# Issuing an output projection in four quarter-width pieces between attention steps instead of two halves at one place

## The chip, the cores and the metric

The kernel runs on one core of one Trainium2 chip. The metric is the device time of one execution in microseconds (us), the median of several runs. The engines are TensorE (PE in the rows: matmuls, with PEld its weight loads), VectorE (DVE), ScalarE (ACT), GpSimd (POOL) and SyncE (SP), which here issues transfers. Each engine executes its own list of instructions in order, and the five lists meet only at semaphores.

## The reference

Two decoder layers on 512 tokens of width 1024, in fp32. Layer 0 mixes tokens by gated linear attention, layer 1 by native sparse attention (16 heads in 4 groups, head width 64). After either mixer comes a mixture of 16 experts. The part at issue is the end of layer 1's mixer and its way into the experts' router:

```python
def nsa_mixer(x, w_in, ..., w_out):
    ...
    o = gb[..., 0:1] * o_cmp + gb[..., 1:2] * o_slc + gb[..., 2:3] * o_win
    ...                                  # o: (B, S, 1024), three branches of attention
    return o @ w_out

for i in range(DEPTH):
    h = gla_mixer(x, ...) if i % 2 == 0 else nsa_mixer(x, ...)
    x = layer_norm(DN_ALPHA * x + h, ln_g[i, 0], ln_b[i, 0])
    f = moe_ffn(x, w_router, ...)        # first step: s = sigmoid(x @ w_router)
    x = layer_norm(DN_ALPHA * x + f, ln_g[i, 1], ln_b[i, 1])
```

## The kernel before, in words

**Tiles.** The 512 tokens are four tiles of 128, numbered 0 to 3. fp32 products are emulated: every operand is split into a high and a low fp16 part, and a product is three matmuls (high by high, high by low, low by high).

**Attention steps.** `nsa_attn` walks a list `order` of 32 steps (tile, group, branch). Steps 0 to 7 are token tile 3, 8 to 15 tile 2, 16 to 23 tile 1, 24 to 31 tile 0. At step i the loop issues `begin(i + 2)`, the scores of the step after next (L1459, L1460: one PSUM bank for each block of keys; when a new tile starts also `cmp_scores`, L1439 to L1446), then for every second step `cmp_pv` (L1494 to L1497, the compressed branch), then `pv` (L1480 to L1485, probabilities by values). `combine` (L1504 to L1516) scales each result by its gate and sums the branches into the tile's output `o`, on VectorE, with the last addition (L1516) on GpSimd for tiles 1 to 3. The probabilities are exponentials by ScalarE (L1427 to L1463) whose low halves VectorE makes (L1435). The buffer `ott`, through which the second and third branch are added, exists once.

**What is filled in.** When a tile's last step is done, its output projection is put in a list `fill`, with the step at which it falls due; the table `ATTN_FILL` holds these steps, one entry for each tile. Three kinds of function are filled in:
- `tr` transposes `o` (TensorE, then the split into fp16 halves oT by ScalarE, L231, and VectorE, L232).
- `out_proj(t, half)` multiplies oT by the 1024 x 1024 output weight, of which one "unit" is 256 columns: units 0 and 1 are the first half of the result's columns, 2 and 3 the second. A unit is the 24 matmuls of `proj_moving` (L256 to L258). After the second unit of a half VectorE adds the residual from PSUM into `r` (L420) and takes the statistics of that half (L291). After the second half follows the layer norm: L310 to L316 on numbers of one column, L302 on both halves, and L303 on both halves, which writes the tile's new rows.
- `finish(t)` is `turn` (eight transposes of the new rows, L273, and their split into xt, L231 and L232) and `score` (the router's logits, L441 to L443: 24 matmuls with 16 columns).

**Priority.** A scheduler may move an instruction a little within an engine's list; the rows in the section on the change show the lists as they come out.

**After attention.** Tile 1's `finish` and all of tile 0's projection belong to the opening of the expert layer, whose weights are split on ScalarE (L178) and VectorE (L180) from the last attention steps on, as they arrive (transfers issued by SyncE at L166 into the buffers that `pv` has released).

The weights' inner loop of one unit:

```python
for k in range(KT):                      # KT = 8
    s = slice(k * 256, (k + 1) * 256)
    nc.tensor.matmul(out, xt[0][:, k], w[0][:, s], start=(k == 0), stop=False)
    nc.tensor.matmul(out, xt[0][:, k], w[1][:, s], start=False, stop=False)
    nc.tensor.matmul(out, xt[1][:, k], w[0][:, s], start=False, stop=(k == KT - 1))
```

Of the kernel before, what the change touches and what calls it, by code (L numbers as in the profile page):

```python
# [34 lines left out]
OUT_POOL = (0, 1), (1, 1), (2, 1)  # L35
PRELUDE = ("r0 r1 o0 t2 r2 oa s2 ob rt rs c0 t3 s3 r3 c1 xb",
           "r0 r1 xa o0 t2 oa s2 r2 rt ob rs c0 t3 s3 r3 c1 xb")
ATTN_FILL = {3: (9, 11, 11, 14), 2: (17, 18, 19, 23), 1: (25, 28, 33), 0: (32,)}
AHEAD = 2
HOT_BY = "ddp"  # L40
UNIT_BY = "dddppppppp"
# [18 lines left out]
class Trunk:  # L60
# [344 lines left out]
    def out_proj(self, t, half, post=True, us=(0, 1)):  # L405
        nc = self.nc
        w, lng, lnb = self.op
        if half == 0:
            self.r = self.xtile(f"r{t}")
            self.bn = self.tmp([P, 2, 6], F32, "bn", 4)  # L410
        r = self.r
        if us[0] == 0:
            self.op_ps = self.bank()
        ps = self.op_ps
        for u in us:
            self.proj_moving(ps[:, u * 256:(u + 1) * 256], w[half * 2 + u], self.oT[t])
        if us[-1] == 0:
            return
        hs = slice(half * 512, half * 512 + 512)
        nc.vector.scalar_tensor_tensor(r[:, hs], ps, IWS / ALPHA, self.x[t][:, hs], op0=OP.mult, op1=OP.add)  # L420
        self.ln_stats(r, half)
        if half == 1:
            self.ln_ins = self.layer_norm(r, lng, lnb)
            self.x[t] = r
            if post:
                self.later(lambda: self.finish(t))
# [989 lines left out]
    def nsa_attn(self, T, pool, early, rest, kcA, kcB, vc, kA, kB, V, VF, qA, qB, gate):  # L1416
# [20 lines left out]
        def cmp_scores(t):  # L1437
            cs = self.bank()
            nc.tensor.matmul(cs.rearrange("p (h q) -> p h q", h=4), self.identb,  # L1439
                             self.cmt[:, t][:, None, :].to_broadcast([P, 4, P]), start=True, stop=False,  # L1440
                             skip_group_check=True)
            for g in range(4):
                gs = slice(g * 32, (g + 1) * 32)
                nc.tensor.matmul(cs[gs], kcA[:, gs], qa(g, t), start=False, stop=False, skip_group_check=True,
                                 tile_position=(0, g * 32))
                nc.tensor.matmul(cs[gs], kcB[:70, gs], qb(g, t), start=False, stop=(g == 3), skip_group_check=True,  # L1446
                                 tile_position=(0, g * 32))
            pc = T([P, S], "pf", F32, 3)
            nc.scalar.activation(pc, cs, AF.Exp)
            pch = T([P, 2, S], "pch", F16, 2)  # L1450
            split(pch[:, 0], pch[:, 1], pc)
            return pch
# [19 lines left out]
        def pv(t, g, b, ph):  # L1472
            ob = self.bank()
            for h in range(4):
                hs = slice(h * P, (h + 1) * P)
                o0 = ob[:, h * 65:(h + 1) * 65]
                exact = t < NT - 1
                if exact:
                    pf = ph[:, t].rearrange("p i q -> p (i q)").bitcast(F32)
                    nc.tensor.matmul(o0, pf[:, hs], VF[b][t][:, g], start=True, stop=(t == 0))  # L1480
                last = t if exact else t + 1
                for j in range(last):
                    nc.tensor.matmul(o0, ph[:, j, 0, hs], V[b][j][:, g, 0:65], start=(j == 0 and not exact), stop=False)
                    nc.tensor.matmul(o0[:, :64], ph[:, j, 0, hs], V[b][j][:, g, 65:129], start=False, stop=False)
                    nc.tensor.matmul(o0, ph[:, j, 1, hs], V[b][j][:, g, 0:65], start=False, stop=(j == last - 1))  # L1485
            return ob

        def cmp_pv(g, pch):
            gs = slice(g * 32, (g + 1) * 32)
            ob = self.bank()  # L1490
            for h in range(4):
                hs = slice(h * P, (h + 1) * P)
                o0 = ob[:, h * 65:(h + 1) * 65]
                nc.tensor.matmul(o0, pch[gs, 0, hs], vc[gs, 0:65], start=True, stop=False, tile_position=(g * 32, 0))  # L1494
                nc.tensor.matmul(o0[:, :64], pch[gs, 0, hs], vc[gs, 65:129], start=False, stop=False,
                                 tile_position=(g * 32, 0))
                nc.tensor.matmul(o0, pch[gs, 1, hs], vc[gs, 0:65], start=False, stop=True, tile_position=(g * 32, 0))  # L1497
            return ob

        def combine(t, g, i, ob, o, first):  # L1500
            cf = T([P, 4], "ocf", F32, 4)
            den = ob[:, 64:260:65]
            if i == 0:
                nc.vector.tensor_scalar(cf, den, 1e-30, None, op0=OP.max)  # L1504
                den = cf
            nc.vector.reciprocal(cf, den)
            nc.vector.tensor_mul(cf, cf, gate[:, t, g * 4:(g + 1) * 4, i])
            og = o[:, g * 256:(g + 1) * 256].rearrange("p (h d) -> p h d", h=4)
            v = ob[:, :260].rearrange("p (h d) -> p h d", h=4)[:, :, 0:64]
            cb = cf[:, :, None].to_broadcast([P, 4, 64])  # L1510
            if first:
                nc.vector.tensor_mul(og, v, cb)
            else:
                tt = T([P, 4, 64], "ott", F32, OTT)
                nc.vector.tensor_mul(tt, v, cb)
                (nc.gpsimd if t else nc.vector).tensor_add(og, og, tt)  # L1516
# [5 lines left out]
        def begin(i):  # L1522
            if i < len(order):
                t, g, b = order[i]
                if g == 0 and b == 0:
                    if t < 3:
                        pch[t] = cmp_scores(t)
                    o[t] = self.row("o")
                ph[i] = scores(t, g, b)

        fill = []
        begin(0)
        begin(1)
        for i, (t, g, b) in enumerate(order):
            begin(i + 2)
            if i in REST_AT:
                for j in range(REST_AT.count(i)):
                    rest[0]()
                    rest = rest[1:]
            if t < 3 and b == 0:  # L1540
                combine(t, g, 0, cmp_pv(g, pch[t]), o[t], True)
            combine(t, g, 1 + b, pv(t, g, b, ph.pop(i)), o[t], t == 3 and b == 0)
            self.pump()
            if i == REST_AT[-1]:
                self.drain()
                ph_, self.ph = self.ph, pool
                early.close()
                self.hl["a"] = self.ctx.enter_context(self.tc.tile_pool(name="wa1", bufs=1, side="right",
                                                                        reuse_waits="tile"))
                self.ph = ph_  # L1550
                self.out_proj_begin([], *self.ln_params(2))
                units = [self.fetch_aside(u) for u in range(3)]
            if i in SPLIT_AT:
                by = SPLIT_BY[SPLIT_AT.index(i)]
                self.op[0].append(self.split(units.pop(0), (), nc.gpsimd if by == "p" else None))
                if i == SPLIT_AT[0]:
                    units.append(self.fetch_aside(3))
            if i == CMP_AT:
                pch[3] = cmp_scores(3)
            if i == 7:  # L1560
                for h in range(4):
                    combine(3, h, 0, cmp_pv(h, pch[3]), o[3], False)
            for f in [f for f in fill if f[0] <= i]:
                fill.remove(f)
                f[1]()
            if i == len(order) - 3:
                self.moe_ahead(1)
            if g == 3 and b == 1:
                def tr(t=t):
                    self.oT[t] = self.transpose_split(o[t], f"oT{t}")  # L1570
                at = ATTN_FILL[t]
                fill.append((at[0], tr))
                if t:
                    fill.append((at[1], lambda t=t: self.out_proj(t, 0)))
                    fill.append((at[2], lambda t=t: self.out_proj(t, 1, False)))
                if t > 1:
                    fill.append((at[3], lambda t=t: self.finish(t)))
        self.table_of(AF.Silu, self.exp_ins)
        for _, f in fill:
            f()  # L1580
# [112 lines left out]
```

## Time and profile before

| | |
|---|---|
| time, median of 3 runs | 957.69 us (957.1 to 959.45) |
| the profiled execution | 958.76 us, span 956.7 us |
| mean granted TensorE clock | 0.965 of full speed |
| busy: TensorE, its weight loads | 92%, 76% |
| busy: VectorE, ScalarE, GpSimd | 78%, 58%, 33% |

The span runs from the first to the last instruction on the chip. Shares are of the span. A busy TensorE means that some matmul is on it. The stretch at issue, from the projection of tile 3 to that of tile 1, lies between 650 and 736 us of the span. Times in the rows are us from the start of the span unless marked ns.

### The profile page before, as it was taken

The numbers are of one execution on the slowest core, as the hardware profiler recorded it, in microseconds if no ns is written. First come the engines' busy times: TensorE is split into PE (matmuls) and PEld (weight loads), VectorE is DVE, ScalarE is ACT, GpSimd is POOL, SyncE is SP. The second block draws the span as 40 slices with busy tenths as digits, with TensorE's granted clock in tenths as the row PEclk, the third lists the DMA queues.
The fourth block names the chain that finished last, engine by engine and source line by source line (L and its number), as shares of the span: only waits on it lengthen the run. The fifth ranks groups of instructions, "written<-read, shape, count | busy, mean of one in ns | idle before, by whom it ended". The sixth has DMA issues, their size and how long they took to land. (4 is left out here: it accounts for less than half of the span.)

```text
span 956.7 us, 26589 instructions
## 1 busy us (share of the span) xinstructions
PE 879.4 (92%) x11218; PEld 722.4 (76%) x11218; DVE 743.5 (78%) x1662; ACT 557.6 (58%) x1178; POOL 313.9 (33%) x353
## 2 busy tenths in 40 slices
PE   6999999996799999879989998999999669999994
PEld 2468888876798889648978886768788568888871
DVE  5972226889899999878678774688777899999967
ACT  4823334424499999713643527775444539999940
POOL 0210021003444331550154524543431258723153
PEclk9999999998899999989999999979999879999997
DMA  8652322072399997951322001120005549999683
GB/s 287 257 210 76 122 89 89 2 307 90 131 367 415 367 377 283 233 178 45 134 89 89 1 3 45 39 97 1 2 2 203 238 176 372 392 382 376 242 155 111
DMA packets 29277, 169.19 MB, mean 177 GB/s; under 512 B 3520, under 2 KB 4160, under 8 KB 12640
## 3 DMA queue, kind: packets, MB, share of 16 engines
q1 hardware_dynamic: 23168, 144.49, 40.1%
q0 software_dynamic: 3072, 12.72, 6.0%
q10 hardware_dynamic: 2912, 10.23, 2.8%
q8 instruction: 90, 1.47, 0.6%
q14 instruction: 35, 0.29, 0.1%
HBM read 153.91 MB, written 13.50 MB: 175 GB/s over the span
## 5 line engine op out<-in xcount | busy, mean ns | idle before, releaser
L851 POOL TENSOR_SCALAR ohe<-icap,rt_px 128x96 f16<-128x96 f32 x112 | 113.1, 1025 | 134.1 <-PE bank L940 125.5
L180 DVE SCALAR_TENSOR_TENSOR whl<-wsu,whl 128x512 f16<-128x512 f32 x192 | 127.0, 711 | 2.9 <-ACT whl L178 2.7
L180 DVE SCALAR_TENSOR_TENSOR whl<-wst,whl 128x512 f16<-128x512 f32 x116 | 75.4, 701 | 68.7 <-ACT whl L178 68.7
L178 ACT ACTIVATE whl<-wsu 128x512 f16<-128x512 f32 x192 | 106.7, 624 | 3.2 <-PE bank L258 3.2
L862 PE MATMUL bank<-ohe,xs 128*128 128x96 f16 x2048 | 99.4, 212 | 6.7 <-DVE ohe L851 5.5
L178 ACT ACTIVATE whl<-wst 128x512 f16<-128x512 f32 x144 | 80.8, 624 | 35.8 <-PE bank L249 9.8
L862 PEld LDWEIGHTS <-xs 128*128 128x128 f16 x2048 | 94.9, 101 | 7.3 <-DVE ohe L851 4.5
L180 DVE SCALAR_TENSOR_TENSOR wha<-wst,wha 128x512 f16<-128x512 f32 x144 | 93.8, 701 | 3.0 <-ACT wha L178 3.0
L256 PE MATMUL bank<-whl,xt 128*128 128x256 f16 x320 | 88.1, 275 | 6.9 <-ACT xt L231 6.9
L257 PE MATMUL bank<-whl,xt 128*128 128x256 f16 x320 | 88.1, 275 | 0.0
L258 PE MATMUL bank<-whl,xt 128*128 128x256 f16 x320 | 87.4, 274 | 0.1
L178 ACT ACTIVATE wha<-wst 128x512 f16<-128x512 f32 x144 | 79.7, 623 | 3.5 <-DMA wst<-moe 3.5
L937 PE MATMUL bank<-xh,whl 128*128 128x96 f16 x576 | 75.2, 206 | 0.0
L935 PE MATMUL bank<-xh,whl 128*128 128x96 f16 x576 | 75.2, 206 | 0.0
L936 PE MATMUL bank<-xh,whl 128*128 128x96 f16 x576 | 75.2, 206 | 0.0
L258 PE MATMUL bank<-whl,oT 128*128 128x256 f16 x256 | 69.6, 273 | 1.6 <-DVE oT L232 1.6
L256 PE MATMUL bank<-whl,oT 128*128 128x256 f16 x256 | 69.7, 273 | 0.5 <-ACT oT L231 0.5
L257 PE MATMUL bank<-whl,xT 128*128 128x256 f16 x256 | 69.8, 273 | 0.0
L258 PE MATMUL bank<-whl,xT 128*128 128x256 f16 x256 | 69.8, 273 | 0.0
L256 PE MATMUL bank<-whl,xT 128*128 128x256 f16 x256 | 69.8, 273 | 0.0
L257 PE MATMUL bank<-whl,oT 128*128 128x256 f16 x256 | 69.7, 273 | 0.0
L936 PE MATMUL bank<-xh,wha 128*128 128x96 f16 x448 | 61.5, 210 | 0.9 <-PEq L1003 0.9
(408 smaller groups left out, 2760.2 us busy)
## 6 DMA issues: line engine op xcount, KB each, us to landing
wsu<-moe SPq DMA_DIRECT2D x54, 1024.0 KB, 7.9
wst<-moe SPq DMA_DIRECT2D x42, 1024.0 KB, 7.6
wst<-gla_in SPq DMA_DIRECT2D x11, 1024.0 KB, 4.8
yslots<-y ACTq DMA_DIRECT2D x26, 384.0 KB, 7.3
wst<-nsa_in SPq DMA_DIRECT2D x9, 1024.0 KB, 5.0
wst<-gla_out SPq DMA_DIRECT2D x4, 1024.0 KB, 4.7
wha<-nsa_out SPq DMA_DIRECT2D x4, 1024.0 KB, 4.9
xs<-xT SPq DMA_DIRECT2D x4, 512.0 KB, 6.9
```

Source lines behind the costliest of these rows:

```text
L178: self.hi_ins = nc.scalar.activation(hl[:, 0, s], st[:, s], AF.Copy, scale=WS)
L180: nc.vector.scalar_tensor_tensor(hl[:, 1, s], st[:, s], WS, hl[:, 0, s], op0=OP.mult, op1=OP.subtract)
L256: nc.tensor.matmul(out, xt[0][:, k], w[0][:, s], start=(k == 0), stop=False)
L257: nc.tensor.matmul(out, xt[0][:, k], w[1][:, s], start=False, stop=False)
L258: nc.tensor.matmul(out, xt[1][:, k], w[0][:, s], start=False, stop=(k == KT - 1))
L851: eng.tensor_scalar(part[e][0][:, t], self.icap, self.px[:, t, e:e + 1], None, op0=OP.is_equal)
L862: nc.tensor.matmul(banks[half][:, j * CAP:(j + 1) * CAP], xs[t][:, i, k * P:(k + 1) * P], oh[:, t], start=(j == 0 and t == self.order[0] a ...
L935: nc.tensor.matmul(o, w[0][:, s], xh[:, 0, k], start=(k == 0), stop=False)
L936: nc.tensor.matmul(o, w[1][:, s], xh[:, 0, k], start=False, stop=False)
L937: nc.tensor.matmul(o, w[0][:, s], xh[:, 1, k], start=False, stop=(k == KT - 1))
```

## The change

The table gets six entries for tiles 3, 2 and 1 in place of four or three: when `tr` is due, when each of the four units is due, and when `finish` is due. `out_proj` may now be called with one unit at a time: the row buffer `r` and the statistics buffer `bn` are taken with the first unit, and the PSUM bank of a half is kept from its first unit to its second. Tile 3's units fall due at steps 10 to 13 instead of all at 11, and its `finish` at 15 instead of 14; tile 2's at 18 to 21 instead of two at 18 and two at 19, `finish` at 24 instead of 23; tile 1's at 27, 28, 30, 31 instead of two at 28 and two behind the last step. No instruction is added or removed.

```diff
-ATTN_FILL = {3: (9, 11, 11, 14), 2: (17, 18, 19, 23), 1: (25, 28, 33), 0: (32,)}
+ATTN_FILL = {3: (9, 10, 11, 12, 13, 15), 2: (17, 18, 19, 20, 21, 24), 1: (25, 27, 28, 30, 31), 0: (32,)}
     def out_proj(self, t, half, post=True, us=(0, 1)):
         nc = self.nc
         w, lng, lnb = self.op
-        if half == 0:
+        if half == 0 and us[0] == 0:
             self.r = self.xtile(f"r{t}")
             self.bn = self.tmp([P, 2, 6], F32, "bn", 4)
         r = self.r
                 at = ATTN_FILL[t]
                 fill.append((at[0], tr))
-                if t:
-                    fill.append((at[1], lambda t=t: self.out_proj(t, 0)))
-                    fill.append((at[2], lambda t=t: self.out_proj(t, 1, False)))
+                for j in range(4 if t else 0):
+                    fill.append((at[1 + j], lambda t=t, j=j: self.out_proj(t, j // 2, False, (j % 2,))))
                 if t > 1:
-                    fill.append((at[3], lambda t=t: self.finish(t)))
+                    fill.append((at[5], lambda t=t: self.finish(t)))
```

On TensorE, the difference between the two lists where tile 3's new rows (r_11036 before) are turned, ahead of the scores of step 17. In these rows ph are probabilities, kA and qA keys and queries, xt the turned rows:

```order
 L1485 LDWEIGHTS ph
 L1485 MATMUL bank<-V_7052,ph 128x65
-L273 MATMUL bank<-identf,r_11036 128x128 x8
-L441 LDWEIGHTS xt_11365
-L441 MATMUL bank<-wrs,xt_11365 128x16
-L442 LDWEIGHTS xt_11365
-L442 MATMUL bank<-wrs,xt_11365 128x16
 L1459 LDWEIGHTS kA_7048
 L1459 MATMUL bank<-qA_7065,kA_7048 128x512
```

The same eight transposes (the rows are r_10972 after the change) and the first two matmuls of the score stand after the change ahead of the scores of step 18, which is the scores of step 17 and the `pv` of step 15 later:

```order
 L1485 LDWEIGHTS ph
 L1485 MATMUL bank<-V_7056,ph 128x65
+L273 MATMUL bank<-identf,r_10972 128x128 x8
+L441 LDWEIGHTS xt_11413
+L441 MATMUL bank<-wrs,xt_11413 128x16
+L442 LDWEIGHTS xt_11413
+L442 MATMUL bank<-wrs,xt_11413 128x16
 L1459 LDWEIGHTS kA_7047
 L1459 MATMUL bank<-qA_7066,kA_7047 128x512
```

The whole group has moved by one step, while the last unit of tile 3's projection moved from `pv` of step 11 to `pv` of step 13, two steps later.

On VectorE, after the change, the list from the end of tile 2's layer norm (L303) to the split of the turned rows (L232, xt_11985); the rows between are combines of attention results (ocf, ott, o):

```order
L303 SCALAR_TENSOR_TENSOR r_11613<-r_11613,lnst,lnb 128x512 x2
L1507 TENSOR_TENSOR ocf<-ocf,gate 128x4
L1504 TENSOR_SCALAR ocf<-bank 128x4
L1515 TENSOR_TENSOR ott<-bank,ocf 128x256
L1506 RECIPROCAL ocf<-ocf 128x4
L1506 RECIPROCAL ocf<-bank 128x4
L1507 TENSOR_TENSOR ocf<-ocf,gate 128x4 x2
L1512 TENSOR_TENSOR o<-bank,ocf 128x256
L1515 TENSOR_TENSOR ott<-bank,ocf 128x256
L232 TENSOR_TENSOR xt_11985<-bank,xt_11985 128x512
L1516 TENSOR_TENSOR o<-o,ott 128x256
L232 TENSOR_TENSOR xt_11985<-bank,xt_11985 128x512
```

Before the change one L1515 stood between the same L303 and the first L232; now there are two, and a GpSimd addition that reads the one buffer `ott` has to come between them.

## Rows read from the trace of the kernel before

**Rows 1.** Windows: window, its length; busy of PE, PEld, DVE, ACT, POOL; clock; DMA.

```profile
634.00:645.00 11.00, 11.00 (x86) 8.41 (x85) 9.89 (x32) 7.49 (x15) 5.40 (x7) 0.50 0.00 0
645.00:650.00 5.00, 5.00 (x53) 3.98 (x53) 5.00 (x10) 3.80 (x8) 1.85 (x2) 0.84 0.02 5
650.00:736.00 86.00, 85.50 (x969) 71.15 (x969) 65.42 (x197) 36.32 (x68) 25.73 (x34) 1.00 0.08 31
736.00:752.00 16.00, 13.34 (x133) 10.90 (x131) 13.75 (x29) 13.96 (x26) 5.02 (x3) 1.00 1.01 424
```

**Rows 2.** Lines, 650 to 736: count | busy, mean ns | idle before, releaser.

```profile
L420 DVE SCALAR_TENSOR_TENSOR r<-bank,r 128x512 f32<-128x512 f32 x6 | 4.1, 689 | 12.9 <-PE bank L258 12.9
```

**Rows 3.** PE's timeline near tile 3's turn: start, duration, instruction [idle before, releaser].

```profile
663.66 0.38 PE L1459 MATMUL bank<-qA,kA 128*128 128x512 f16 x1
...
668.60 0.33 PE L1480 MATMUL bank<-VF,ph 128*128 128x65 f32 x2
...
670.25 0.38 PE L1439 MATMUL bank<-cmt,identb 128*128 128x512 bf16 x1
...
674.31 1.07 PE L273 MATMUL bank<-identf,r 128*128 128x128 f32 x8
...
675.70 0.38 PE L1459 MATMUL bank<-qA,kA 128*128 128x512 f16 x1
...
676.57 0.22 PE L1480 MATMUL bank<-VF,ph 128*128 128x65 f32 x1
```

**Rows 4.** DVE's timeline: residual (L420), layer norm's end (L303) of tiles 3, 2, 1, 0.

```profile
663.86 0.69 DVE L420 SCALAR_TENSOR_TENSOR r<-bank,r 128x512 f32<-128x512 f32 x1 [2.28 <-PE bank L258]
...
670.28 1.87 DVE L303 SCALAR_TENSOR_TENSOR r<-r,lnst,lnb 128x512 f32<-128x512 f32 x2
...
700.33 0.69 DVE L420 SCALAR_TENSOR_TENSOR r<-bank,r 128x512 f32<-128x512 f32 x1 [3.88 <-PE bank L258]
...
707.54 1.75 DVE L303 SCALAR_TENSOR_TENSOR r<-r,lnst,lnb 128x512 f32<-128x512 f32 x2
...
743.79 1.41 DVE L303 SCALAR_TENSOR_TENSOR r<-r,lnst,lnb 128x512 f32<-128x512 f32 x2
...
755.39 0.68 DVE L420 SCALAR_TENSOR_TENSOR r<-bank,r 128x512 f32<-128x512 f32 x1
...
760.58 1.41 DVE L303 SCALAR_TENSOR_TENSOR r<-r,lnst,lnb 128x512 f32<-128x512 f32 x2
```

**Rows 5.** PE's timeline: tile 1's last two units begin; tile 1's turn.

```profile
730.25 0.27 PE L256 MATMUL bank<-whl,oT 128*128 128x256 f16 x1
...
744.69 1.29 PE L273 MATMUL bank<-identf,r 128*128 128x128 f32 x8 [1.26 <-DVE r L303]
745.82 0.27 PE L256 MATMUL bank<-whl,oT 128*128 128x256 f16 x1
```

**Rows 6.** PE's timeline near tile 2's turn.

```profile
705.11 0.38 PE L1439 MATMUL bank<-cmt,identb 128*128 128x512 bf16 x1
...
710.10 1.07 PE L273 MATMUL bank<-identf,r 128*128 128x128 f32 x8
...
712.47 0.32 PE L1480 MATMUL bank<-VF,ph 128*128 128x65 f32 x1
...
717.18 1.10 PE L1480 MATMUL bank<-VF,ph 128*128 128x65 f32 x8
718.12 0.38 PE L1459 MATMUL bank<-qA,kA 128*128 128x512 f16 x1
```

**Rows 7.** DVE's timeline: a combine that waits for GpSimd's addition.

```profile
714.19 0.42 DVE L1515 TENSOR_TENSOR ott<-bank,ocf 128x256 f32<-128x256 f32 x1 [1.18 <-POOL o L1516]
```

**Rows 8.** DVE's timeline at the end of attention.

```profile
733.58 1.90 DVE L180 SCALAR_TENSOR_TENSOR wha<-wst,wha 128x512 f16<-128x512 f32 x3 [1.26 <-ACT wha L178]
735.69 0.69 DVE L420 SCALAR_TENSOR_TENSOR r<-bank,r 128x512 f32<-128x512 f32 x1 [0.21 <-PE bank L258]
```

**Rows 9.** PE's timeline just before the clock was at half.

```profile
632.71 0.40 PE L1459 MATMUL bank<-qA,kA 128*128 128x512 f16 x1 [0.94 <-ACT ph L1463]
```

## The prediction

> **What bounds the kernel now.** I read the windows first, cut where the change begins and ends. From 650 to 736 us TensorE is busy 85.50 of 86.00 us at a granted clock of 1.00 [rows 1]: in this stretch TensorE is the bound, and the two waits left come to 0.50 us. VectorE is busy 65.42 of the same 86.00. Behind 736 the picture changes: TensorE is busy 13.34 of 16.00, the transfers fill the DMA engines (share 1.01), VectorE has 13.75 and ScalarE 13.96 [rows 1]. There the layer norms, the router and the arriving expert weights set the pace.
>
> Second, the view by lines of VectorE in that stretch. The largest idle time stands ahead of the residual additions (L420): 12.9 us, all of it released by the projection's last matmul (L258) [rows 2]. That is the idle time the change works on: VectorE stands while TensorE does 48 or 96 projection matmuls in a row. The reader is to see that TensorE has no idle time beside it; TensorE is working while VectorE waits.
>
> Third, the timelines around the places where TensorE takes something from the layer norm: the transposes (L273) of the new rows of tiles 3 and 2. Before, they wait for nothing: tile 3's layer norm ends at 670.28 + 1.87 = 672.15 [rows 4], the transposes begin at 674.31 [rows 3], 2.16 us of slack. Tile 2's ends at 707.54 + 1.75 = 709.29 [rows 4] against 710.10 [rows 6], 0.81 us of slack. Tile 1's turn lies behind attention and does wait, 1.26 us [rows 5].
>
> **The change part by part.** The lists of before and after hold the same instructions; only their order changes, on four engines. SyncE's list is unchanged, and `out_proj` and `finish` issue no transfers.
>
> *Splitting the projection.* One unit costs TensorE (735.69 − 0.21 − 730.25) / 2 = 2.62 us [rows 5, 8], wherever it stands. TensorE was not waiting, so moving units saves it nothing. A half's PSUM bank is now kept over one attention step between its two units; in that time the lists show four other banks taken (three for scores, one for `pv`), so nothing should wait for one. Cost 0, hidden by TensorE's own work; if a bank were short, TensorE would stand for the rest of a `pv`, up to 1.65 us [rows 3].
>
> *Term A: tile 3's turn.* The last unit now ends two steps later, the turn stands only one step later. What lies between them on TensorE after the change: the stretch from `cmp_scores` to the transposes as before, 674.31 − 670.25 = 4.06; the scores of step 17, 676.57 − 675.70 = 0.87; and a `pv` of tile 2, 670.25 − 668.60 = 1.65 [rows 3]: 6.58 us. The layer norm must fit into that. From L420 at 663.86 to L303's end at 672.15 it took 8.29 us, with attention's own VectorE work interleaved [rows 4], and the list after has the same number and kinds of operations between. L420 starts 0.20 us behind the end of the unit (663.66 [rows 3] to 663.86). From L303's end to TensorE's next work behind the transposes go 0.62 us, read at tile 1, where the transposes wait: 743.79 + 1.41 = 745.20 [rows 4] to 745.82 [rows 5]. So TensorE is through at 0.20 + 8.29 + 0.62 = 9.11 us behind the last unit. Unhindered it would be there at 6.58 plus the transposes and the beginning of the score with its small wait, 675.70 − 674.31 = 1.39 [rows 3], of which two score matmuls (0.06) come in both: 7.91. **A = 9.11 − 7.91 = +1.2 us.** The slack of 2.16 us has become a wait.
>
> *Term B: tile 2's turn.* It moves by one step, its last unit from step 19 to step 21, again two. Cover on TensorE: 710.10 − 705.11 = 4.99; the scores and `cmp_pv` of the next step, 712.47 − 710.10 = 2.37 less 1.39 for the turn in between, 0.98; a `pv` of tile 0, 718.12 − 717.18 = 0.94 [rows 6]: 6.91 us, and 1.33 for the transposes. The layer norm took 709.29 − 700.33 = 8.96 us [rows 4]; the list after has one 128x512 split and one small operation fewer in it, some 0.7 us, so about 8.2; by tile 3's row it would be 7.8. I take 8.0. 0.21 + 8.0 + 0.62 = 8.83 against 8.24: **+0.6 us**. Then the rest of the score needs the low half of the turned rows (L232). Before it the list after shows two multiplications into `ott` with GpSimd's addition between. This order stands in the trace once, with a wait of 1.18 us [rows 7]. TensorE has some other work there (0.5 us of scores), so I count **+0.4 us**, with bounds of 0 and 1.18.
>
> *Term C: the end of attention.* The last `pv` now stands behind one more unit and ends 2.62 us later, at 732.87 instead of 730.25 [rows 5]. Its combine was done at 733.58 − 1.26 = 732.32, 2.07 us behind the `pv` [rows 8, 5]; now, with the step before already cleared, 1.6 to 2.1 us behind it, at 734.4 to 734.9. In the list it stands ahead of three weight splits (L180) that started at 733.58 and take 1.90 [rows 8]. They now end at 736.3 or later, and the residual of tile 1 (L420), at 735.69 before [rows 8], starts 0.6 us later. Then VectorE runs nearly without a break to tile 1's layer norm end, for which TensorE waits [rows 5]. VectorE's slack in that stretch (16.00 − 13.75 [rows 1]) can take some back: **+0.5 us**, bounds 0 and 1.1.
>
> *What gets better.* VectorE's 12.9 us of idle time [rows 2] shrinks, since combines and additions now lie beside the units. That is worth nothing while TensorE is gap-free. At most the two small waits, 0.50 us [rows 1], could vanish; I see no reason why.
>
> Sum: 1.2 + 0.6 + 0.4 + 0.5 = +2.7 us. On the profiled execution, 958.76 to 961.5 us; that execution is 1.1 us over the median 957.69, so against the median I forecast **960.4 us**. Bounds: a layer norm as short as tile 0's, 760.58 + 1.41 − 755.39 = 6.60 us [rows 4], removes A and B's first part; with nothing lost elsewhere and the small waits gone the sum is −0.5. With 8.96 us for both tiles, A is 1.9 and B 1.5 + 1.18, with C 1.1: +5.7.
>
> **The clock.** At 632.71 TensorE waited 0.94 us [rows 9], and from 634 to 645 the granted clock was 0.50, that is 1.2 GHz, in 645 to 650 0.84 [rows 1]. A wait like A's lies behind 674 in the changed kernel. But the wait of 1.26 us at 744.69 [rows 5] stands in a stretch at 1.01 DMA share whose clock stayed 1.00 [rows 1]. So one wait of this size does not decide it. The Trainium skill ("TensorE: Matmul & The Clock Gate", section "A second HAM failure mode: psum-queue depth-cycling") describes a kernel whose clock oscillates because TensorE idles briefly between groups of matmuls. This trace agrees at 634 and not at 745; by the page the interleaved order, with new small waits, would be slower than the sum above. That makes it a rival, below.
>
> **The rivals.**
> 1. *The layer norm fits* (chance 0.18). VectorE has fewer combines queued when the last unit ends, and the norm is as short as tile 0's 6.60 us. Then 957.2 to 959, no change that can be told. Against it: the list between L420 and L303 is as long as before.
> 2. *The half clock* (0.10, slower). If the new waits at tiles 3 and 2 set off what follows 632.71, a stretch like that of 634 to 646.6 (11.00 us and 5.00 x 0.32 us of rows 1) runs at 1.2 GHz and costs about half its length, 6.3 us: 960.4 + 6.3 = 966.7. It decides from the first fall of the clock between 674 and 736. For it: a wait of 0.94 us stood ahead of the half clock once. Against it: TensorE's two waits in the stretch were harmless, and so was 1.26 at 744.69.
> 3. *VectorE was the hidden bound* (0.12, faster). If the idle time of VectorE could be turned into an earlier end, up to 12.9 us [rows 2] would be won: 944.8 at the utmost. The point from which it shows is 2.9 us (0.3%). The Trainium skill ("Perfetto Trace Analysis", section "Optimization Strategy") says that interleaving regimes with different most-contended engines may improve performance; here that speaks for the change. Rows 1 don't agree: in this stretch only 0.50 us of TensorE is free, so a gain has to come from behind 736, for instance if the expert weights' splits started earlier. I see only that they start later (term C).
>
> **How the numbers follow.** 0.3% of 957.69 is 2.9 us, about what a measurement of this kernel can tell from no change: up to 960.6 counts as the same, from 954.8 down as faster. The case of the sum (0.60) reaches from 958.9 to 962.5 and is cut by that line just above its middle: 0.32 same, 0.28 slower. With rival 1 (0.18) same is 0.50; with rival 2 slower is 0.38; faster is 0.12. The range leaves out rival 2 and most of rival 3, which are 0.2 together: 956.6, where the no-wait case with the lost small waits ends, to 963.4, the sum's upper bound of +5.7.
>
> **What would show it.** In the profile after: TensorE waits for VectorE's L303 ahead of the transposes, about 1.2 us near 677 (A) and 0.6 near 712 (B); a wait ahead of the score's L443 for L232 of about 0.4; the three weight splits starting 0.8 later than attention's shift explains, and tile 1's turn 0.5 (C). TensorE's busy time in the stretch is unchanged, the clock 1.00, VectorE's wait for L258 ahead of L420 far below 12.9. The prediction is wrong if the transposes wait for nothing (rival 1), if the clock reads 0.50 in a window between 674 and 736 (rival 2), or if the stretch behind 736 is shorter (rival 3).

## The result and the profile after

The changed kernel takes 973.67 us (median of 4 executions, 964.94 to 977.13) against 958.17 us for the kernel before on the same chip: a ratio of 1.0142 (95% interval 1.0109 to 1.0174), slower by about 14 us by that ratio and by 15.5 us by the medians. One of the four executions took only 964.94 us. The forecast was 960.4 us, in a range up to 963.4. The profiled execution took 971.6 us, with a span of 969.8 and a mean granted clock of 0.951.

The windows of the changed kernel, first the two that answer to [rows 1], then the stretch cut at its own marks (670.44 and 716.28 are the starts of `cmp_scores`, L1439, which stood at 670.25 and 705.11 before; 749.19 is the first transpose of tile 0, at 735.49 before). Columns as in [rows 1]:

```profile
650.00:736.00 86.00, 82.57 (x824) 66.09 (x822) 58.79 (x170) 32.80 (x61) 23.98 (x32) 0.86 0.00 1
736.00:752.00 16.00, 14.62 (x142) 12.68 (x140) 11.35 (x33) 7.04 (x13) 1.27 (x2) 1.00 0.57 188
...
670.44:681.00 10.56, 8.87 (x108) 6.09 (x106) 10.16 (x30) 5.51 (x11) 2.76 (x3) 0.97 0.01 2
681.00:701.00 20.00, 20.00 (x146) 15.90 (x145) 8.47 (x25) 5.99 (x11) 4.73 (x7) 0.51 0.00 1
701.00:716.28 15.28, 15.28 (x161) 12.94 (x159) 6.04 (x18) 4.72 (x9) 4.08 (x6) 1.00 0.01 3
716.28:749.19 32.91, 31.74 (x328) 26.61 (x325) 25.78 (x83) 11.98 (x21) 6.84 (x10) 0.95 0.21 65
```

The line to look at is that of 681 to 701. TensorE is busy for all of its 20.00 us, so no idle time is to be seen there, but the granted clock is 0.51: 1.2 GHz instead of 2.4. Work of some 10.2 us takes 20. What stands ahead of it is in TensorE's timeline (the two marks, and the transposes that answer to [rows 3, 5 and 6]):

```profile
670.44 0.38 PE L1439 MATMUL bank<-cmt,identb 128*128 128x512 bf16 x1
...
678.38 0.63 PE L273 MATMUL bank<-identf,r 128*128 128x128 f32 x4 [1.19 <-DVE r L303]
679.51 0.63 PE L273 MATMUL bank<-identf,r 128*128 128x128 f32 x4 [0.51 <-DVE r L303]
...
716.28 0.38 PE L1439 MATMUL bank<-cmt,identb 128*128 128x512 bf16 x1
...
724.54 1.88 PE L273 MATMUL bank<-identf,r 128*128 128x128 f32 x8 [1.17 <-DVE r L303]
...
749.19 1.04 PE L273 MATMUL bank<-identf,o 128*128 128x128 f32 x8
...
758.80 1.29 PE L273 MATMUL bank<-identf,r 128*128 128x128 f32 x8 [1.27 <-DVE r L303]
```

And in VectorE's, the residual and the layer norm's end for tiles 3 and 2, and the end of attention, which answer to [rows 4 and 8]:

```profile
670.64 0.69 DVE L420 SCALAR_TENSOR_TENSOR r<-bank,r 128x512 f32<-128x512 f32 x1 [1.30 <-PE bank L258]
...
677.50 1.87 DVE L303 SCALAR_TENSOR_TENSOR r<-r,lnst,lnb 128x512 f32<-128x512 f32 x2
...
716.48 0.69 DVE L420 SCALAR_TENSOR_TENSOR r<-bank,r 128x512 f32<-128x512 f32 x1 [1.25 <-PE bank L258]
...
723.29 1.85 DVE L303 SCALAR_TENSOR_TENSOR r<-r,lnst,lnb 128x512 f32<-128x512 f32 x2
...
747.99 1.89 DVE L180 SCALAR_TENSOR_TENSOR wha<-wst,wha 128x512 f16<-128x512 f32 x3
749.80 0.69 DVE L420 SCALAR_TENSOR_TENSOR r<-bank,r 128x512 f32<-128x512 f32 x1
```

VectorE's idle time ahead of L420 fell as forecast, from 12.9 us [rows 2] to 4.9 (the same six additions, which reach to 750 us here):

```profile
L420 DVE SCALAR_TENSOR_TENSOR r<-bank,r 128x512 f32<-128x512 f32 x6 | 4.1, 689 | 4.9 <-PE bank L258 4.9
```

Between the marks the time went here. From `cmp_scores` of tile 1 on TensorE has the same work in both kernels. The last mark before the change is this row of its timeline:

```profile
735.49 1.04 PE L273 MATMUL bank<-identf,o 128*128 128x128 f32 x8
```

| stretch | before | after | difference |
|---|---|---|---|
| 670.25 to 705.11; 670.44 to 716.28 | 34.86 | 45.84 | +10.98 |
| 705.11 to 735.49; 716.28 to 749.19 | 30.38 | 32.91 | +2.53 |
| 735.49 to 744.69 (tile 1's turn); 749.19 to 758.80 | 9.20 | 9.61 | +0.41 |

The waits at tile 3 (1.19 + 0.51, less the 0.25 of before) are 1.45 of the 10.98; the half clock, some 20.00 x (1 − 0.51) = 9.8 us, is the rest, within 0.3 us. In the second stretch 1.17 − 0.25 is waiting, and a clock of 0.95 over 32.91 us is another 1.6.

### The profile page after: what moved, and what is told of

The parts are those of the page before. It is cut to its first block, busy times and chain, and to the rows that moved or that the text cites. A ratio compares the mean times of both kernels' runs of the same rounds, so it can differ in the third digit from the quotient of the medians.

```text
span 969.8 us, 26588 instructions
## 1 busy us (share of the span) xinstructions
PE 892.7 (92%) x11218; PEld 728.5 (75%) x11218; DVE 745.2 (77%) x1662; ACT 558.6 (58%) x1178; POOL 314.3 (32%) x353
## 5 line engine op out<-in xcount | busy, mean ns | idle before, releaser
L258 PE MATMUL bank<-whl,oT 128*128 128x256 f16 x256 | 70.6, 276 | 2.1 <-DVE oT L232 2.1
L256 PE MATMUL bank<-whl,oT 128*128 128x256 f16 x256 | 70.8, 277 | 0.5 <-ACT oT L231 0.5
L257 PE MATMUL bank<-whl,oT 128*128 128x256 f16 x256 | 70.7, 276 | 0.0
```

## The experiments

Two theories stood against each other. **W**: TensorE's waits for the layer norm let the clock fall, and the half clock behind them is most of the loss. **T**: the spreading of the units itself, without long runs of projection matmuls, lets the clock fall, whatever waits. In the diffs the table is in its six-entry form; in the kernels that keep an old place, units of a half with equal entries are issued together, and the table of before reads `3: (9, 11, 11, 11, 11, 14), 2: (17, 18, 18, 19, 19, 23), 1: (25, 28, 28, 33, 33)` with the units and turns in the order of before. Each run was timed beside the kernel before on the same chip.

| run | median us (lowest to highest) | before | ratio (95% interval) |
|---|---|---|---|
| e1 | 965.15 (962.23 to 973.65) | 959.21 | 1.0084 (1.0050 to 1.0118) |
| e2 | 966.53 (958.82 to 972.78) | 959.21 | 1.0068 (1.0043 to 1.0094) |
| e3 | 964.24 (963.59 to 965.19) | 959.21 | 1.0048 (1.0035 to 1.0061) |
| e4 | 961.64 (959.95 to 963.10) | 959.21 | 1.0027 (1.0018 to 1.0036) |
| e5 | 960.68 (959.01 to 962.11) | 959.54 | 1.0011 (1.0000 to 1.0022) |
| e6 | 960.66 (958.51 to 962.47) | 959.54 | 1.0017 (1.0006 to 1.0028) |
| e7 | 963.89 (959.64 to 971.75) | 959.54 | 1.0052 (1.0032 to 1.0073) |
| e8 | 976.88 (965.92 to 978.78) | 959.54 | 1.0144 (1.0103 to 1.0186) |
| e9 | 968.66 (965.56 to 972.45) | 959.83 | 1.0085 (1.0063 to 1.0107) |
| e10 | 967.83 (965.87 to 968.63) | 959.83 | 1.0087 (1.0068 to 1.0105) |
| e11 | 961.41 (960.05 to 965.94) | 959.83 | 1.0023 (1.0006 to 1.0039) |
| e12 | 965.11 (962.94 to 967.08) | 958.64 | 1.0063 (1.0047 to 1.0080) |

**e1: tile 3's turn one step later.**

```diff
-ATTN_FILL = {3: (9, 10, 11, 12, 13, 15), ...
+ATTN_FILL = {3: (9, 10, 11, 12, 13, 16), ...
```

> The change with one number different: tile 3's finish is due at step 16 instead of 15, so the scores, cmp_pv and pv of one more step (about 3 us of TensorE) cover its layer norm. Theory W (the wait of 1.19 + 0.51 us for L303 ahead of tile 3's transposes sets off the half clock from 681 to 701 us): no wait ahead of tile 3's transposes, granted clock 1.00 from 675 to 720, the time 961 to 964 us, some 10 below the changed kernel. Theory T (units spread one by one leave TensorE with too few long projection runs, and the clock falls whatever waits): the clock still reads 0.50 for 10 us or more between 675 and 705, time 968 to 976. The wait ahead of tile 2's transposes (about 1.2 us) stays in both.

The wait ahead of the transposes went, but another came in its place, ahead of the rest of the score. The timeline row, and the two windows between the marks:

```profile
686.26 0.18 PE L443 MATMUL bank<-wrs,xt 128*128 128x16 f16 x1 [1.52 <-DVE xt L232]
```

```profile
672.74:709.30 36.56, 34.79 (x412) 28.16 (x409) 25.10 (x72) 15.58 (x30) 12.00 (x16) 1.00 0.01 2
709.30:741.80 32.50, 30.59 (x327) 25.47 (x325) 25.77 (x83) 11.98 (x21) 6.79 (x10) 1.00 0.19 74
```

The profiled execution has a clock of 1.00 throughout and pays 1.70 and 2.12 us for waits alone; three of the seven executions took 968 us or more at lower mean clocks. So W's wait was not taken away cleanly here, and the run doesn't decide.

**e2: tile 3 alone** as in the change, tiles 2 and 1 as before.

```diff
-ATTN_FILL = {3: (9, 11, 11, 11, 11, 14), ...
+ATTN_FILL = {3: (9, 10, 11, 12, 13, 15), ...
```

> Only tile 3's places are those of the change; tiles 2 and 1 keep whole halves at the places of before. Theory W: the same wait of 1.2 + 0.5 us ahead of tile 3's transposes and the same half clock behind it; time 968 to 973, nearly the whole loss. Theory T: one tile's units spread are a quarter to a third of the effect, and tile 2's halves of 5.2 us come soon after, so the half clock is short or missing: 960 to 963.

The same waits of 1.19 and 0.51 us, and behind them this window:

```profile
680.00:692.00 12.00, 12.00 (x93) 9.56 (x91) 5.84 (x18) 4.54 (x9) 3.26 (x5) 0.50 0.01 1
```

Eight of twelve executions took 965.9 us or more, at mean clocks of 0.950 to 0.959, the other four 958.8 to 962.6 at 0.960 to 0.965: with the same waits the clock seems to fall in most executions and not in all. The median is a little under W's 968. The place is tile 3's, as W says.

**e3: tile 3 undone**, tiles 2 and 1 as in the change (the reverse of e2's edit).

> The reverse: tiles 2 and 1 in single units as in the change, tile 3 in one run of 96 matmuls with finish at step 14, as before. Theory W: no wait and no half clock near 674 to 700; left are tile 2's wait (about 1.2 us, with about 3 us of half clock behind it, seen at 725 to 728 in the changed kernel) and the 0.4 us at the end of attention: 960 to 963. Theory T: a fall of the clock for 10 us or more somewhere between 690 and 740, 966 or more.

Nothing near tile 3; behind tile 2's wait of 1.18 us a short fall:

```profile
716.50:723.00 6.50, 6.50 (x52) 5.05 (x50) 5.76 (x16) 2.83 (x7) 1.36 (x2) 0.50 0.01 3
```

The time is a little above W's 963, and all five executions agree within 1.6 us. The half clock cost 3.2 us here, not the 1.6 of the changed kernel's profile.

**e4: nothing spread, the turn one step early.** The kernel before with

```diff
-ATTN_FILL = {3: (9, 11, 11, 11, 11, 14), ...
+ATTN_FILL = {3: (9, 11, 11, 11, 11, 13), ...
```

> The kernel before with one number different: tile 3's finish due at step 13 instead of 14, units in whole halves as before, so nothing is spread. The layer norm then ends about 1.9 us behind the point where TensorE wants the rows (672.15 against 670.25 in the trace of before). Theory W: a wait of 1.5 to 2.3 us ahead of tile 3's transposes and a half clock of 10 to 20 us behind it: 965 to 971. Theory T: the wait alone, without the spreading, costs its own 2 us: 960 to 961, clock 1.00 to 720.

The waits, and the window over the whole stretch:

```profile
671.05 0.63 PE L273 MATMUL bank<-identf,r 128*128 128x128 f32 x4 [0.75 <-DVE r L303]
672.19 0.63 PE L273 MATMUL bank<-identf,r 128*128 128x128 f32 x4 [0.51 <-DVE r L303]
```

```profile
655.00:736.75 81.75, 80.24 (x903) 66.57 (x901) 60.76 (x187) 32.23 (x60) 23.27 (x32) 1.00 0.08 30
```

T's numbers nearly came out: 1.26 us of waiting cost only about 2.6 us and the clock held. By W alone this had to be slower; either W is wrong or the wait was too short.

**e5: tile 3 spread, no wait.** The kernel before with

```diff
-ATTN_FILL = {3: (9, 11, 11, 11, 11, 14), ...
+ATTN_FILL = {3: (9, 10, 11, 12, 13, 17), ...
```

> Tile 3's units spread one by one as in the change, its finish due at step 17 so that two more steps cover the layer norm and the split of the turned rows; tiles 2 and 1 as before. Theory W (waits of TensorE for the layer norm or the split set off the half clock): no wait over 0.3 us between 655 and 700 us, granted clock 1.00 there, time within 2 us of the kernel before, 957 to 961. Theory T (the spreading itself lets the clock fall): half clock for 7 us or more in the stretch in most executions, 963 to 970, with a spread of several us between executions as in the change.

```profile
672.59:738.20 65.61, 65.10 (x737) 53.71 (x735) 48.69 (x156) 27.33 (x51) 18.59 (x26) 1.00 0.10 39
```

The same stretch in the kernel before:

```profile
670.25:735.49 65.24, 64.73 (x741) 53.70 (x737) 47.27 (x149) 27.48 (x51) 20.28 (x28) 1.00 0.10 37
```

Both windows reach from `cmp_scores` to tile 0's transposes: 65.61 us against 65.24 before, at a clock of 1.00, and all twelve executions lie within 3.1 us. T is out: spread units without a wait leave the clock alone. They bring nothing either.

**e6: tile 1 alone** (term C). The kernel before with `1: (25, 27, 28, 30, 31)`.

> Only tile 1's places are those of the change; tiles 3 and 2 as before. That is term C by itself: pv of the last step ends one unit (2.6 us) later, the weight splits start about 0.8 us later, tile 1's turn 0.4 us later: 959.5 to 960, clock 1.00 from 660 to 750. By theory T the spreading of tile 1's units would bring a half clock before 750 and 963 or more.

The two marks in its timeline:

```profile
735.79 1.04 PE L273 MATMUL bank<-identf,o 128*128 128x128 f32 x8
...
745.39 1.29 PE L273 MATMUL bank<-identf,r 128*128 128x128 f32 x8 [1.27 <-DVE r L303]
```

From tile 0's transposes to tile 1's turn go 9.60 us in its trace against 9.20 before, 0.40 more, with the clock at 1.00; the timing, +0.6 to +2.7 us, is a little more than that.

**e7: tile 2 alone.** The kernel before with `2: (17, 18, 19, 20, 21, 24)`.

> Only tile 2's places are those of the change; tiles 3 and 1 as before. Waits of about 1.2 us ahead of tile 2's transposes and 0.6 us ahead of the rest of its score, less the 0.25 us of before: 1.6 to 2.1 us. Theory W: some executions have a half clock of 3 to 7 us right behind the wait (near 718), so 961 to 964. Theory T: half clock already during the units, between 685 and 705, 964 or more.

Both forecast waits are there, in a profiled execution without a fall:

```profile
717.33 1.38 PE L273 MATMUL bank<-identf,r 128*128 128x128 f32 x8 [1.17 <-DVE r L303]
...
720.81 0.18 PE L443 MATMUL bank<-wrs,xt 128*128 128x16 f16 x1 [0.63 <-DVE xt L232]
```

Its stretch from L1439 to tile 0's transposes takes 32.55 us against 30.38: +2.2 us without any half clock. Executions reach from 959.6 us at a mean clock of 0.967 to 971.8 at 0.952, so here too the clock seems to fall in some.

**e8: nothing spread, the turn two steps early.** As e4 with 12 in the place of 13.

> The kernel before with tile 3's finish due at step 12 instead of 14 (the run with 13 had waits of 0.75 + 0.51 us and no fall of the clock in its profile), units in whole halves. The wait ahead of the transposes grows to 2.5 to 3.5 us. Theory W: now the clock falls to 0.50 for 7 to 20 us behind it, 965 to 971. Theory T (the spreading is what matters): the wait costs only itself, 961.5 to 963, clock 1.00 from 660 to 735.

The wait, and the window of the half clock:

```profile
672.48 2.22 PE L273 MATMUL bank<-identf,r 128*128 128x128 f32 x8 [3.54 <-DVE r L303]
```

```profile
671.30:705.30 34.00, 32.77 (x235) 23.92 (x235) 15.89 (x40) 12.25 (x23) 7.86 (x11) 0.50 0.00 1
```

One number of the kernel before was changed, nothing is spread, and the loss is as large as that of the whole change: 3.54 us of waiting, 34 us of half clock, more than W's 7 to 20 us and 965 to 971. With e4 and e2 this makes a row by size: 1.26 us, no execution above 963.1; 1.70 us, most above 965.9; 3.54 us, all six above it. The row doesn't hold everywhere. In the trace of before stand two waits of about 3 us, and the clock behind either is back at full within some 5 us. The waits in TensorE's timeline, and the windows:

```profile
498.23 0.40 PE L1289 MATMUL bank<-ident,QT 128*128 128x128 f16 x4 [3.10 <-DVE QT L1283]
...
578.86 1.92 PE L1337 MATMUL bank<-ident,QT 128*70 128x128 f16 x16 [2.97 <-DVE QT L1329]
```

```profile
499.00:504.00 5.00, 5.00 (x48) 4.24 (x49) 5.00 (x9) 1.21 (x2) 5.00 (x7) 0.66 0.48 200
578.00:582.00 4.00, 3.14 (x20) 2.27 (x21) 1.00 (x3) 2.65 (x5) 0.00 (x0) 0.57 0.10 16
```

**e9 and e10: the wait filled with useless work.** In the changed kernel (e9) ahead of the turns of tiles 3 and 2, and in e8's kernel (e10, with 16 matmuls, for tile 3 only):

```diff
-                    fill.append((at[5], lambda t=t: self.finish(t)))
+                    def turn_late(t=t):
+                        ps = self.bank()
+                        for _ in range(8):
+                            nc.tensor.matmul(ps, kA[0][:, 0, 0:P], qa(0, 0), start=True, stop=True)
+                        self.finish(t)
+                    fill.append((at[5], turn_late))
```

> The changed kernel plus useless work: ahead of the transposes of tiles 3 and 2 stand eight more 128x512 matmuls each (products of keys and queries into a bank that nothing reads), about 1.75 us of TensorE each, as long as the waits of 1.70 and 1.2 us that they fill. Theory W (it is TensorE standing still that lets the clock fall): the clock stays at 1.00 from 650 to 735, the work costs nothing beyond the waits, and the time drops to 962 to 965, with executions within 3 us of each other, although 16 matmuls were added. Theory T, or a cause that has nothing to do with the waits: half clock as in the changed kernel, 972 to 978.

> The kernel before with tile 3's turn two steps early (which gave 976.9 us with a wait of 3.54 us and 34 us of half clock behind it), with 16 useless 128x512 matmuls (about 3.5 us) in the place of the wait. Theory W: no half clock behind 671, 962 to 964: the 3.5 us are paid as work and nothing else. If it is the early place of the turn and not the idle time: 970 or more.

The windows over the stretch, of e9 and then of e10:

```profile
655.00:743.19 88.19, 87.35 (x967) 71.10 (x965) 63.93 (x190) 35.11 (x66) 25.26 (x34) 1.00 0.07 24
```

```profile
655.00:741.71 86.71, 85.85 (x945) 69.95 (x943) 63.38 (x191) 34.18 (x64) 24.98 (x34) 1.00 0.08 28
```

The clock is 1.00 in both, and both are faster than the kernels without the extra work (973.67 and 976.88). But both are some 4 us slower than W's sum, and e9's executions lie 6.9 us apart, not within 3. The view of TensorE's waits behind 760 shows a wait that came to 0.2 us at most in the kernels without added instructions, on TensorE's own sequencer behind a jump (L1003) in the expert layer; e9's row, then e10's (total, count, longest):

```profile
PE bank L862 <- PEq L1003: 3.5, 1, 3.5
```

```profile
PE bank L862 <- PEq L1003: 2.2, 1, 2.2
```

e9's profiled execution is the slowest of its six, 972.45 us, and its clock fell outside the stretch too: it reads 0.57 from 632 to 652, a fall that begins ahead of all that was changed, and 0.57 from 794 to 798, behind the sequencer's wait.

**e12: the same filling with fewer instructions.** Two fp32 matmuls of 512 columns instead of eight fp16 ones:

```diff
-                        for _ in range(8):
-                            nc.tensor.matmul(ps, kA[0][:, 0, 0:P], qa(0, 0), start=True, stop=True)
+                        for _ in range(2):
+                            nc.tensor.matmul(ps, self.identf, self.x[0][:, 0:512], start=True, stop=True)
```

> The run with the filled waits again, but with two fp32 matmuls of 512 columns ahead of each turn in place of eight fp16 ones: four instructions more in all, not sixteen, since the first version had a new wait of 3.52 us on TensorE's sequencer far behind the place (L862 behind L1003, near 794 us), which no kernel without added instructions had. Theory W: no half clock from 650 to 735; the time 962 to 966, and if the added instructions caused that wait, it is smaller or gone. If the cause of the loss is not TensorE's idle time: 972 or more.

```profile
655.00:742.02 87.02, 86.42 (x947) 69.98 (x945) 64.29 (x190) 34.41 (x64) 24.89 (x34) 1.00 0.08 29
```

```profile
L1579 PE MATMUL bank<-r,identf 128*128 128x512 f32 x8 | 3.9, 609 | 0.0
```

The first row is the window, the second the added work in the view by lines (its four matmuls count as eight there): 3.9 us busy. The sequencer's wait is gone, the clock is 1.00 in the stretch, and all six executions have a mean clock of 0.964 or 0.965 and lie between 962.9 and 967.1. Nearly the same schedule as the change, with 3.9 us more work on the engine that is the bound, is 8.6 us faster than the change by the medians. From `cmp_scores` of tile 1 to tile 0's transposes, where the kernel before takes 65.24 us, e12 and e9 take the same:

```profile
672.52:742.02 69.50, 68.90 (x744) 55.11 (x742) 50.33 (x155) 27.60 (x51) 18.52 (x26) 1.00 0.10 36
673.68:743.19 69.51, 68.67 (x753) 55.19 (x751) 50.30 (x155) 27.61 (x51) 18.53 (x26) 1.00 0.09 30
```

That is 4.3 us more, of which the added work is 3.9 and 3.8: between the marks the filling costs little more than itself.

**e11: tiles 3 and 2 spread, with later turns.** Table `3: (9, 10, 11, 12, 13, 17), 2: (17, 18, 19, 20, 21, 26)`, tile 1 as before.

> The change with its waits removed by later turns: units of tiles 3 and 2 one by one, finish of tile 3 at step 17 and of tile 2 at 26, tile 1 as before. Theory W: clock 1.00 from 655 to 735, no TensorE wait over 0.3 us there, time within 0.2% of before (958 to 961): the spreading is worth nothing, since TensorE had no idle time to fill. Rival 3 of the prediction (VectorE's idle time is worth something once the waits are out of the way): 956 or less.

A little above W's 958 to 961, and far from rival 3's 956: +0.6 to +3.7 us. Small waits of 0.25, 0.26 and 0.37 us are left between 720 and 724, and behind them a short fall, as these windows show:

```profile
655.00:724.00 69.00, 67.83 (x780) 54.50 (x777) 53.39 (x156) 29.51 (x56) 24.69 (x33) 1.00 0.01 2
724.00:728.00 4.00, 4.00 (x43) 3.39 (x42) 3.03 (x14) 0.18 (x1) 0.28 (x1) 0.57 0.00 0
```

## Why the prediction was wrong, point by point

**What bounds the stretch: right.** TensorE was gap-free before, and spreading its units saved nothing: e5 with no wait is within 0.0 to 0.2% of before. Rival 3 (VectorE's idle time as a reserve) is out: 8.0 us of it were filled in the changed kernel and no run became faster. The Trainium skill ("Perfetto Trace Analysis", section "Optimization Strategy") has interleaving as a possible gain where the most-contended engine changes; in e5 and e11 it gave none, since here TensorE was the contended one all along.

**Term A: right in place, nearly right in size.** Forecast +1.2 us; measured 1.19 + 0.51 of waiting less 0.25, 1.45. The layer norm took 677.50 + 1.87 − 670.64 = 8.73 us, not 8.29; 0.31 of the difference is a single L302, 1.05 us instead of 0.74.

**Term B: mis-sized.** Forecast 0.6 + 0.4; e7 shows 1.17 − 0.25 and 0.63 of waits, 1.55 us, and 2.2 us in its stretch with everything (in the changed kernel's own profile the second wait doesn't show; TensorE is at half clock there, and late itself). The layer norm took 723.29 + 1.85 − 716.48 = 8.66 us where I took 8.0, from 8.96 before. The two operations that I had left out (an L1435 and an L1504) are indeed gone and none came in, but the norm is only 0.30 us shorter: the second L302 took 1.06 us instead of 0.74 and the two L303 1.85 instead of 1.75.

**Term C: right.** Forecast +0.5, measured +0.41 at tile 1's turn in the change and +0.40 in e6 alone.

**The clock: the step that failed.** I wrote that "one wait of this size does not decide it", from the wait of 1.26 us at 744.69 whose clock stayed at 1.00, put the clock at nothing in the sum, and gave rival 2 a chance of 0.10 and a price of 6.3 us. A wait of 1.70 us in two parts, in another place, was followed by 20 us of half clock, a price of 9.8 us; rival 2's own sign, 0.50 in a window between 674 and 736, is what came. That the waiting sets it off, and not the spreading or the place of the turn, is shown by four runs: with the wait and no spreading the clock falls (e8), with spreading and no wait it doesn't (e5), and with the wait filled by useless work it doesn't either, in either kernel (e10, where 0.51 us of the wait is left, and e12). That is one profiled execution of each; the times of the others agree with it. The Trainium skill ("TensorE: Matmul & The Clock Gate", section "A second HAM failure mode: psum-queue depth-cycling") names short idle times between groups of matmuls as a cause of lost clock; these runs agree, and by it I should have weighed rival 2 higher. The price came from one fall alone, 12.6 us long; the falls in these runs are 3 to 34 us long. The trace of before had others, such as those behind 498 and 578, which the prediction doesn't use.

**The sum.** With A 1.45, B 2.2 and C 0.4 the change costs about 4 us by its waits; the half clock adds about 10 in the profiled execution. e12, where waits are replaced by 3.9 us of work and the clock holds, is +6.5 us by its medians, some 2 more than 3.9 and C make. Little of that remainder lies in the stretch: its two windows are +4.3 us there, and tile 1's turn adds 0.4. Its mark at 672.52 comes 2.27 us later than 670.25, and 1.72 of these are there already at tile 3's own transposes (646.57 against 644.85), ahead of all that differs: in the profiled execution the rest stands mostly outside the stretch. In the forecast's range the lower end doesn't follow from its sum: −0.5 us from 957.69 is 957.2, not 956.6.

**What stays open.** Why the same wait is followed by a fall in most executions and not in all (e2, e7; only one execution of each was profiled, so that is inferred from the times); why 1.26 us at tile 1's turn, and 1.52 and 1.17 us at tiles 3 and 2 in e1's profile, were followed by none, and 1.18 us in e3 and 0.88 us in three parts in e11 by one; and what sets the length of a fall, since 3.10 us was followed by a short one and 3.54 us by 34 us.

## What to carry to other kernels

Before moving work between steps on the engine that is the bound, list every place where that engine takes something from another, with its slack: here one step of cover was given up for an idle time on VectorE that cost nothing. A TensorE wait of 1 to 2 us must not be priced at its own length: in this kernel the granted clock behind one was at half for up to 20 us, and TensorE's busy share didn't show it (20.00 of 20.00 us), only the clock column did. If a wait can't be avoided, useless matmuls in it are a cheap test of whether the clock is what it costs.

## What the runs showed of the hardware that was not expected

- Executions of one kernel spread far more when it has such a wait: 958.82 to 972.78 us in e2, against 959.01 to 962.11 in e5, which differs by the place of the turn only.
- The fall need not lie within the wait, and it lasts. In the changed kernel the second wait ends at 679.51, the clock reads 1.00 until 680 and 0.51 from 681 to 701, while TensorE has no idle time at all. In e8, with one long wait, it reads 0.50 from 671.5 on, ahead of the wait's end at 672.48.
- With sixteen matmuls added at 680 and 718 us a sequencer wait of 3.5 us stands on the first expert matmuls behind a jump (2.2 us with 16 in one place), over 70 us later; the version with two long matmuls in the place of eight had none. What joins the two was not shown.
